# A hybrid SSD and attention block: head products of a group in one cluster, short matmuls first in every other chunk

## The chip, the cores and the metric

The kernel runs on one core of a Trainium2 chip, as one launch. The metric is the device time of that launch in microseconds (us). Weights stay in HBM in float32 and are streamed once.

## The reference

One decoder block over 256 tokens of width 2048, all in float32:

```python
h = rmsnorm(x, norm_w[l])
proj = h @ w_in[l]                       # z | xBC | dt | q k v | g_attn | g_merge
xbc = silu(causal_dwconv(xbc, conv_w[l], conv_b[l]))          # 4 taps
xs, Bm, Cm = jnp.split(xbc, xbc_pts, axis=-1)
dt = softplus(dt_raw + dt_bias[l]); A = -exp(A_log[l])
# ssd_scan, one chunk of 256 tokens, 8 groups of 8 heads of 64 channels:
cum = jnp.cumsum(dt_ * Ah, axis=1)
decay = jnp.exp(jnp.where(causal, cum[l] - cum[s], -jnp.inf))
w = (C @ B.T)[group] * decay * dt        # 256 x 256 for each head
y = w @ x_  +  D_skip * x_
y = group_rmsnorm(y * silu(z), ssm_norm_w[l], 8)
y_ssm = y @ w_ssm_proj[l]
y_attn = (moba_attention(q, k, v) * silu(g_attn)) @ w_attn_proj[l]   # 16 heads, causal softmax
mixed = sigmoid(g_ssm) * y_ssm + sigmoid(g_att) * y_attn
x = rmsnorm(x + mixed @ w_out[l], final_norm_w)
```

## The kernel before

**Weights in chunks.** Every weight matrix is cut into blocks of columns, and each block into chunks of 128 x 1024 numbers (`chunks`, line 103). The main loop (line 903) takes one chunk after another, 480 in all (chunk numbers here count from 0 in the order of the loop). A chunk is loaded on SyncE's queue seven chunks ahead (`load`), and split into two rounded halves for exact enough products: whi on ScalarE four chunks ahead (`split_hi`, line 244), wlo = raw - whi on VectorE, called DVE, three chunks ahead (`split_lo`, line 251). There are five buffers for whi and four for wlo, so DVE's split for chunk n+3 waits until TensorE, called PE, has used the wlo of chunk n-1. The activations (h2 and others) stand in two halves as well.

**Two ways to multiply a chunk.** `by_channel` (line 298) has the weights as stationary operand: eight matmuls of whi against both halves of the activations (128x512, long), and then eight of wlo against the upper half alone (128x256, short). All accumulate in PSUM tiles named acc. It serves z, B and C (bc), x, q, k and the attention gate. `by_token` (line 282) has the activations as stationary operand, 12 long matmuls to a chunk; it serves the gates, v and the three output projections.

**Small work between chunks.** After a chunk's matmuls are issued, `step` advances generators by one yield each: those that empty acc (`evac`), one SSD group (`ssd`, one group at a time) and two attention heads (`attn`). Each engine runs its instructions in the order in which they were issued, so a yield is what sets how many chunks lie between a product and its use. A run of such small matmuls between two chunks is called a cluster here.

**One SSD group** (`ssd_task`, line 541): `xtr(t)` transposes x for one half of the tokens (four matmuls into px); `xmul` scales it by dt on DVE; `decay(p)` takes two heads' differences of cum on DVE and their exp on ScalarE (tile e); `emul(p)` multiplies e by the masked C B (cbm) on DVE; `ymm(p)` multiplies two heads into half a PSUM tile yp with weights of 128x64; `yev(q)` empties one yp on DVE. The four pairs of heads are p = 0 to 3. Later steps multiply by the gate z, take the group's norm with a sum over channels on PE (pn) and write y2, which the SSM projection reads.

Pools that matter: four PSUM tiles for all small products (px, pcb, yp, pn and others) in turn; tag e with three buffers, shared with `rstd_start`; separate tiles for the SSD mask, the attention mask (amask) and rsb (the input norm).

Of the kernel before, what the change touches and what calls it, by code (L numbers as in the profile page):

```python
# [10 lines left out]
F32 = mybir.dt.float32  # L11
F32R = mybir.dt.float32r
AF = mybir.ActivationFunctionType
OP = mybir.AluOpType

P = 128
S = 256
# [3 lines left out]
NG = 8  # L21
# [7 lines left out]
NEG = -1e30  # L29
# [97 lines left out]
def hybrid_block(  # L127
# [12 lines left out]
    nc = tc.nc  # L140
    ctx.enter_context(tc.manual_schedule())

    cpool = ctx.enter_context(tc.tile_pool(name="cpool", bufs=1))
# [3 lines left out]
    pool = ctx.enter_context(tc.tile_pool(name="pool", bufs=1))  # L147
# [48 lines left out]
    for c0 in (0, 256):  # L196
# [1 line left out]
            out=mask[:, c0 : c0 + P], in_=mask[:, c0 : c0 + P], pattern=[[1, P]],  # L198
            compare_op=OP.is_ge, fill=0.0, base=0, channel_multiplier=-1,
        )  # L200

    amask = cpool.tile([P, 384], F32, name="amask")
    nc.gpsimd.memset(amask, 0.0)
    for c0 in (0, 256):
        nc.gpsimd.affine_select(
            out=amask[:, c0 : c0 + P], in_=amask[:, c0 : c0 + P], pattern=[[-1, P]],
            compare_op=OP.is_ge, fill=NEG, base=0, channel_multiplier=1,
        )
    dt_tok = cpool.tile([P, 2, HEADS], F32, name="dt_tok")
    pc_tok = cpool.tile([P, 2, HEADS], F32, name="pc_tok")  # L210
    ssq = cpool.tile([P, 2, 5], F32, name="ssq")
# [67 lines left out]
    def mm(dst, a, bb, start, stop):  # L279
        nc.tensor.matmul(dst, a, bb, start=start, stop=stop, skip_group_check=True)  # L280
# [17 lines left out]
    def by_channel(n, accs):  # L298


        b, k0, per, ncol = cks[n]
        name, _, _, _, row, nrows = blocks[b]
        name = "first" if b < 3 else name
        wh, wl = weights(n, False)
        last_k = nrows // P - 1
        order = [(i, c) for i in range(per) for c in range(ncol // P)]
        passes = [[(part, i, c) for i, c in order] for part in range(2)]
        if len(accs) > 1 and k0 + per > last_k:

            passes = [[x for x in p if x[2] // 2 == a] for a in range(len(accs)) for p in passes]  # L310
        for part, i, c in (x for p in passes for x in p):
            k = k0 + i
            a = operand(name, row // P + k)
            dst = accs[c // 2].rearrange("p (c s) -> p c s", c=2)[:, c % 2]
            cs = slice(c * P, (c + 1) * P)
            if part == 0:
                mm(dst, wh[:, i, cs], a.rearrange("p a s -> p (a s)"), k == 0, False)
            else:
                mm(dst[:, S:], wl[:, i, cs], a[:, 0], False, k == last_k)

# [25 lines left out]
    sq = {}  # L346
# [26 lines left out]

    pss = small("pss")

    rsb = cpool.tile([P, S], F32, name="rsb")

    def init_task():

# [126 lines left out]
    def bc_task(g, acc):  # L506
        bc = pool.tile([P, 2, S], F32, tag="bc", name="bc")
        u = pool.tile([P, 2, S], F32, tag="u", name="u", bufs=2)
        fold(u, acc)
        yield  # L510
        jobs = [(bc[:, i], u[:, i], 32 + 8 * i + g) for i in range(2)]
        for job in jobs:
            tap(*job)
        yield from conv(jobs)
        nc.scalar.activation(bc, bc, AF.Silu)
        yield
        yield
        pcb = small("pcb")
        nc.tensor.matmul(pcb[:, :S], bc[:, 0, :P], bc[:, 1, :], start=True, stop=True)  # L519
        nc.tensor.matmul(pcb[:, S:384], bc[:, 0, P:], bc[:, 1, P:], start=False, stop=True, skip_group_check=True)  # L520
        yield
        cbm = pool.tile([P, 384], F32, tag="s", name="cbm", bufs=2)
        nc.vector.tensor_mul(cbm, pcb[:, :384], mask)
        wk["cbm", g] = cbm

    def x_task(i, acc):
# [14 lines left out]
    def ssd_task(g, xs):  # L541
# [12 lines left out]
        def xtr(t):  # L554
            px[t] = small("px")
            for i in range(4):
                nc.tensor.transpose(px[t][:, i * P : (i + 1) * P], xs[:, i, t * P : (t + 1) * P], ident)  # L557
# [12 lines left out]
        yps = {}  # L570

        def decay(p):
            e = es[p] = pool.tile([P, 2, 384], F32, tag="e", name="e", bufs=3)
            for j in range(2):
                h = 2 * p + j
                hh = g * HPG + h
                cbr = cB[h // 4][:, h % 4]
                for st, sl, dst in ((0, slice(0, S), slice(0, S)), (1, slice(P, S), slice(S, 384))):
                    nc.vector.tensor_scalar(  # L579
                        e[:, j, dst], cbr[:, sl], pc_tok[:, st, hh : hh + 1], 0.0, op0=OP.subtract, op1=OP.max  # L580
                    )
            nc.scalar.activation(e, e, AF.Exp, scale=-1.0)  # L582
# [20 lines left out]
        def yev(q):  # L603
            yp = yps.pop(q)
            for i in (2 * q, 2 * q + 1):
                nc.vector.scalar_tensor_tensor(
                    y[:, i], xs[:, i], dsk[:, 4 * g + i : 4 * g + i + 1], yp[:, (i % 2) * S : (i % 2 + 1) * S],
                    op0=OP.mult, op1=OP.add,
                )

        xtr(0)
        decay(0)
        yield
        xmul(0)
        xtr(1)
        emul(0)
        decay(1)
        yield
# [1 line left out]
        emul(1)  # L620
        decay(2)
        yield
        ymm(0)
        ymm(1)
        emul(2)
        yield
        decay(3)
        yield
        yev(0)
        emul(3)  # L630
        yield
        ymm(2)
        ymm(3)
        yield
        yield
        yev(1)
        yield
# [13 lines left out]
        yield  # L651
        a, r = rstd_start(nc, pool, pn[:, :S], DI // NG, epst)
        yield
        rs = pool.tile([P, S], F32, name="rs")
        rstd_newton(nc, rs, a, r)
        yield
        for i in range(4):
# [8 lines left out]

    SC = 128.0 ** -0.5

    def head_task(u, h, q, k, v, og):
        if h == 1:  # L670
            for _ in range(3):
                yield
        ps = small("ps")
        nc.tensor.matmul(ps[:, :P], q[:, h, :P], k[:, h, :P], start=True, stop=True, skip_group_check=True)  # L674
        nc.tensor.matmul(ps[:, P:384], q[:, h, P:], k[:, h, :], start=False, stop=True, skip_group_check=True)  # L675
        yield
        s = pool.tile([P, 384], F32, tag="s", name="s", bufs=2)
        m = pool.tile([P, 8], F32, name="m", bufs=2)
        nc.vector.tensor_add(s, ps[:, :384], amask)
        nc.vector.reduce_max(m[:, 0:1], s[:, :P], axis=mybir.AxisListType.X)  # L680
        nc.vector.reduce_max(m[:, 1:2], s[:, P:], axis=mybir.AxisListType.X)
        nc.vector.tensor_scalar(m[:, 2:4], m[:, 0:2], -SC, None, op0=OP.mult)
        nc.scalar.activation(s[:, :P], s[:, :P], AF.Exp, bias=m[:, 2:3], scale=SC, accum_out=m[:, 4:5])
        nc.scalar.activation(s[:, P:], s[:, P:], AF.Exp, bias=m[:, 3:4], scale=SC, accum_out=m[:, 5:6])
        yield
        yield
        nc.vector.reciprocal(m[:, 6:8], m[:, 4:6])
        nc.vector.tensor_scalar(s[:, :P], s[:, :P], m[:, 6:7], None, op0=OP.mult)
        nc.vector.tensor_scalar(s[:, P:], s[:, P:], m[:, 7:8], None, op0=OP.mult)
        yield  # L690
        pp = small("pp")
        for i in range(3):
            nc.tensor.transpose(pp[:, i * P : (i + 1) * P], s[:, i * P : (i + 1) * P], ident)  # L693
        yield
        p = pool.tile([P, 384], F32, tag="e", name="p", bufs=3)
        nc.scalar.copy(p, pp[:, :384])
        yield
        po = small("po")
        hs = slice(h * P, (h + 1) * P)

        nc.tensor.matmul(po[:, :S], v[:, 0, hs], p[:, : 2 * P], start=True, stop=False, skip_group_check=True)  # L701
        nc.tensor.matmul(po[:, P:S], v[:, 1, hs], p[:, 2 * P :], start=False, stop=True, skip_group_check=True)  # L702
        yield
        while ("ga", u) not in wk:
            yield
        nc.vector.tensor_mul(og[:, h], po[:, :S], wk["ga", u][:, h])
        if h == 3:
            yield
            both = apool.tile([P, 4, 2, S], F32R, tag="act", name="o2")
            nc.scalar.copy(both[:, :, 0], og)  # L710
            yield
            nc.vector.tensor_sub(both[:, :, 1], og, both.bitcast(F32)[:, :, 0])
            o2[u] = both
# [120 lines left out]
    def residual(acc, j, t, c0, c1, slot):  # L834

        js = slice(j * 512 + c0, j * 512 + c1)
        r = wk["xr"][:, t, js]
        nc.vector.tensor_add(r, acc, r)
        sq = pool.tile([P, 512], F32, tag="e", name="sq", bufs=3)
        nc.scalar.activation(sq[:, : c1 - c0], r, AF.Square, accum_out=ssq[:, t, slot : slot + 1])  # L840
        nc.vector.tensor_mul(r, r, wk["fwt"][:, js])

# [103 lines left out]

def rstd_start(nc, pool, ss, n, epst):

    ar = pool.tile([P, 2, ss.shape[-1]], F32, tag="e", name="ar", bufs=3)
    a, r = ar[:, 0], ar[:, 1]  # L950
    nc.scalar.activation(r, ss, AF.Ln, bias=epst, scale=1.0 / n)
    nc.scalar.activation(r, r, AF.Exp, scale=-0.5)
    nc.vector.tensor_scalar(a, ss, 1.0 / n, EPS, op0=OP.mult, op1=OP.add)
    return a, r
# [45 lines left out]
```

## Time and profile before

| | |
|---|---|
| Time, median of 3 runs | 1433.35 us (1433.32 to 1433.42) |
| Profiled execution, its own time | 1433.54 us |
| Span in the profile | 1431.8 us |
| PE busy | 1414.5 us, 99% |
| DVE busy | 940.1 us, 66% |
| ScalarE (ACT) busy | 768.9 us, 54% |
| DMA, mean rate | 191 GB/s |

Busy times of matmuls overlap, since one starts before the one ahead of it has ended. How fast PE gets on is read from the starts of its rows, not from their durations. The profile shows an engine's wait as idle time before a row, in square brackets with the engine and line that ended it.

### The profile page before, as it was taken

What the parts mean: (1) busy time and instruction counts of PE and PEld (TensorE: products, weight loads), DVE (VectorE), ACT (ScalarE), POOL (GpSimd) and SP (SyncE); (2) the same over time, 40 slices, a digit from 0 to 9 for tenths busy, and PEclk for the clock granted to TensorE, in tenths of its full rate; (3) what the DMA queues carried; (4) which work ended last, traced back from release to release, by engine and by line L of the source; (5) the groups of instructions that cost most, each with busy time, mean ns of one, the idle gap of its engine ahead of it and who ended that gap; (6) DMA issues with size and microseconds to landing.
All of it is one profiled execution on the core that took longest, in us unless ns stands there. A gap on an engine that the chain in (4) does not pass through costs nothing.

```text
span 1431.8 us, 19449 instructions
## 1 busy us (share of the span) xinstructions
PE 1414.5 (99%) x7474; PEld 1204.2 (84%) x7474; DVE 940.1 (66%) x1291; ACT 768.9 (54%) x909; POOL 3.8 (0%) x15
## 2 busy tenths in 40 slices
PE   8999999999999999999999999999999999999997
PEld 7888888888888888888888888888888888888886
DVE  7788788777777777876646555555555555655564
ACT  7556667565756565655444345455454454444352
POOL 0000000000000000000000000000000000000000
PEclk9999999999999999999999999999999999999999
DMA  8455646565656565656665655555655566665762
GB/s 309 146 188 186 212 158 208 164 205 177 216 165 215 168 213 169 200 199 205 206 213 191 188 187 167 186 177 162 192 170 174 186 190 195 203 206 191 262 214 84
DMA packets 77068, 273.66 MB, mean 191 GB/s; under 512 B 8432, under 2 KB 8752, under 8 KB 76592
## 3 DMA queue, kind: packets, MB, share of 16 engines
q1 hardware_dynamic: 76400, 271.68, 58.6%
q8 instruction: 58, 0.95, 0.3%
q10 hardware_dynamic: 576, 0.75, 0.2%
q14 instruction: 34, 0.28, 0.1%
HBM read 270.24 MB, written 2.16 MB: 190 GB/s over the span
## 4 chain that ended last, share of the span: by engine, by line
PE 98%; DVE 1%; DMA 0%; ACT 0%; issue 0%; DVEq 0%; SPq 0%
PE acc L280 92%; PE yp L597 2%; PE half L280 1%; PE px L557 0%; PE po L701 0%; PE ps L675 0%; DMA raw<-wpk 0%; PE pp L693 0%; PE pd L406 0%; PE pcb L519 0%; PE ps L674 0%; PE po L702 0%; PE pm L816 0%; PE pn L650 0%; DVE wlo L251 0%; DVE e L586 0%
## 5 line engine op out<-in xcount | busy, mean ns | idle before, releaser
L251 DVE TENSOR_TENSOR wlo<-raw,whi 128x1024 fp32r<-128x1024 f32 (+1 forms) x477 | 581.4, 1222 | 415.5 <-PE acc L280 315.1
L244 ACT CAST whi<-raw 128x1024 fp32r<-128x1024 f32 (+1 forms) x477 | 496.4, 1046 | 497.2 <-PE acc L280 408.1
L280 PE MATMUL acc<-h,whi 128*128 128x512 f32 x1920 | 489.2, 397 | 0.0
L280 PEld LDWEIGHTS acc<-h,whi 128*128 128x128 f32 x1920 | 346.6, 189 | 65.7 <-issue 2.4
L280 PEld LDWEIGHTS acc<-h,wlo 128*128 128x128 f32 x1920 | 261.8, 190 | 19.2
L280 PE MATMUL acc<-h,wlo 128*128 128x256 f32 x1920 | 267.5, 282 | 0.0
L280 PE MATMUL acc<-whi,h 128*128 128x512 f32 x768 | 241.0, 391 | 0.0
L280 PEld LDWEIGHTS acc<-whi,h 128*128 128x128 f32 x768 | 144.2, 188 | 29.7
L280 PE MATMUL acc<-whi,y 128*128 128x512 f32 x512 | 162.9, 393 | 0.0
L280 PE MATMUL acc<-wlo,h 128*128 128x512 f32 x384 | 149.5, 389 | 0.0
L280 PEld LDWEIGHTS acc<-whi,y 128*128 128x128 f32 x512 | 96.1, 188 | 20.8 <-issue 1.0
L280 PE MATMUL acc<-wlo,y 128*128 128x512 f32 x256 | 99.8, 390 | 0.0
L280 PEld LDWEIGHTS acc<-wlo,h 128*128 128x128 f32 x384 | 72.1, 188 | 14.5
L280 PE MATMUL acc<-whi,o 128*128 128x512 f32 x256 | 79.6, 390 | 0.0
L280 PEld LDWEIGHTS acc<-whi,o 128*128 128x128 f32 x256 | 48.1, 188 | 9.9
L280 PEld LDWEIGHTS acc<-wlo,y 128*128 128x128 f32 x256 | 48.1, 188 | 9.5
L582 ACT ACTIVATE e<-e 128x768 f32<-128x768 f32 x32 | 27.1, 848 | 42.8 <-DVE e L579 42.7
L280 PE MATMUL acc<-wlo,o 128*128 128x512 f32 x128 | 49.8, 389 | 0.0
L499 DVE SCALAR_TENSOR_TENSOR xs<-u,colt,xs 128x255 f32<-128x255 f32 (+2 forms) x96 | 40.7, 478 | 2.1 <-ACT xs L492 2.1
L280 PE MATMUL acc<-wlo,m_hi 128*128 128x512 f32 x104 | 40.6, 390 | 0.0
L280 PE MATMUL acc<-whi,m_hi 128*128 128x512 f32 x104 | 40.5, 390 | 0.0
L280 PE MATMUL acc<-whi,m_lo 128*128 128x512 f32 x104 | 40.5, 389 | 0.0
(192 smaller groups left out, 1044.6 us busy)
## 6 DMA issues: line engine op xcount, KB each, us to landing
raw<-wpk SPq DMA_DIRECT2D x479, 512.0 KB, 3.6
cumb<-scratch SPq DMA_DIRECT2D x16, 512.0 KB, 6.1
sig<-gbias SPq DMA_DIRECT2D x8, 512.0 KB, 6.8
xt<-xT SPq DMA_DIRECT2D x8, 256.0 KB, 6.9
xr<-x SPq DMA_DIRECT2D x1, 2048.0 KB, 11.3
out<-xr SPq DMA_DIRECT2D x6, 256.0 KB, 3.6
fwt<-fw SPq DMA_DIRECT2D x1, 1024.0 KB, 12.4
raw<-wpk SPq DMA_DIRECT2D x2, 256.0 KB, 6.3
```

The source lines that it names most:

```text
L244: nc.scalar.copy(his[n][:, h], raws[n][:, h])
L251: nc.vector.tensor_sub(los[n][:, h], r[:, h], his[n].bitcast(F32)[:, h])
L280: nc.tensor.matmul(dst, a, bb, start=start, stop=stop, skip_group_check=True)
L499: nc.vector.scalar_tensor_tensor(dst[:, d:], u[:, : S - d], cw[:, ct, 3 - d : 4 - d], dst[:, d:], op0=OP.mult, op1=OP.add)
L582: nc.scalar.activation(e, e, AF.Exp, scale=-1.0)
L597: nc.tensor.matmul(yp[r, st * P :], xd[:, st, h * 64 : (h + 1) * 64], e[:, j, :S] if st == 0 else e[:, j, S:384], start=(st == 0 and p % 2 ...
```

## The change

1. Both x transposes of a group stand in one cluster, and all four `ymm` as well: four pairs of heads, behind one more yield. The tag e gets a fourth buffer.
2. In `by_channel` every chunk with an odd place in its block does its short matmuls (wlo) first and its long ones after.
3. To make room, the attention mask is written over the SSD mask when the last group has used it (`attn_mask`), and rsb and each group's rs share one buffer.

```diff
@@ by_channel
+        turn = (0, 1) if k0 // per % 2 == 0 else (1, 0)
-        passes = [[(part, i, c) for i, c in order] for part in range(2)]
+        passes = [[(part, i, c) for i, c in order] for part in turn]
...
-                mm(dst, wh[:, i, cs], a.rearrange("p a s -> p (a s)"), k == 0, False)
+                mm(dst, wh[:, i, cs], a.rearrange("p a s -> p (a s)"), k == 0, k == last_k)
@@ init and ssd_task
-    rsb = cpool.tile([P, S], F32, name="rsb")
+    rsb = pool.tile([P, S], F32, tag="rs", name="rsb", bufs=1)
...
-            e = es[p] = pool.tile([P, 2, 384], F32, tag="e", name="e", bufs=3)
+            e = es[p] = pool.tile([P, 2, 384], F32, tag="e", name="e", bufs=4)
...
         xtr(0)
+        xtr(1)
         decay(0)
         yield
         xmul(0)
-        xtr(1)
         emul(0)
         decay(1)
         yield
...
         emul(1)
         decay(2)
         yield
-        ymm(0)
-        ymm(1)
         emul(2)
-        yield
         decay(3)
         yield
+        emul(3)
+        yield
+        yield
+
+        for p in range(4):
+            ymm(p)
+        yield
+        yield
         yev(0)
-        emul(3)
-        yield
-        ymm(2)
-        ymm(3)
-        yield
         yield
         yev(1)
...
-        rs = pool.tile([P, S], F32, name="rs")
+        rs = pool.tile([P, S], F32, tag="rs", name="rs", bufs=1)
@@ masks
+        if g == NG - 1:
+            attn_mask()
...
+    def attn_mask():
+
+        nc.gpsimd.memset(mask, 0.0)
+        for c0 in (0, 256):
+            nc.gpsimd.affine_select(
+                out=mask[:, c0 : c0 + P], in_=mask[:, c0 : c0 + P], pattern=[[-1, P]],
+                compare_op=OP.is_ge, fill=NEG, base=0, channel_multiplier=1,
+            )
...
-        nc.vector.tensor_add(s, ps[:, :384], amask)
+        nc.vector.tensor_add(s, ps[:, :384], mask)
```

On PE, in SSD group 0, from the product pcb of the next group's B and C to the head products yp, before (two of the four pairs stand here, the other two stood three chunks earlier, ahead of pcb):

```order
L519 MATMUL pcb<-bc 128x256
L520 MATMUL pcb<-bc 128x128
L280 MATMUL acc<-h_123,whi 128x512 x8
L280 MATMUL acc<-h_123,wlo 128x256 x8
L280 MATMUL acc<-h_123,whi 128x512 x8
L280 MATMUL acc<-h_123,wlo 128x256 x8
L280 MATMUL acc<-h_123,whi 128x512 x8
L280 MATMUL acc<-h_123,wlo 128x256 x8
L597 MATMUL yp<-e,xd 64x256 x2
L597 MATMUL yp<-e,xd 64x128 x2
L597 MATMUL yp<-e,xd 64x256 x2
L597 MATMUL yp<-e,xd 64x128 x2
```

The same stretch of PE in the changed kernel:

```order
L513 MATMUL pcb<-bc 128x256
L514 MATMUL pcb<-bc 128x128
L272 MATMUL acc<-h_115,wlo 128x256 x8
L272 MATMUL acc<-h_115,whi 128x512 x16
L272 MATMUL acc<-h_115,wlo 128x256 x16
L272 MATMUL acc<-h_115,whi 128x512 x8
L593 MATMUL yp<-e,xd 64x256 x2
L593 MATMUL yp<-e,xd 64x128 x2
L593 MATMUL yp<-e,xd 64x256 x2
L593 MATMUL yp<-e,xd 64x128 x2
L593 MATMUL yp<-e,xd 64x256 x2
L593 MATMUL yp<-e,xd 64x128 x2
```

Two more pairs (four more rows of the same two kinds) follow there; all four pairs now stand where the last two stood, and runs of long and of short matmuls join across chunks.

On DVE, group 0, from the fourth `decay` to its `emul` (the product e<-e,cbm), before:

```order
L579 TENSOR_SCALAR e<-cumb,pc_tok 128x256
L579 TENSOR_SCALAR e<-cumb,pc_tok 128x128
L579 TENSOR_SCALAR e<-cumb,pc_tok 128x256
L579 TENSOR_SCALAR e<-cumb,pc_tok 128x128
L251 TENSOR_TENSOR wlo<-raw,whi 128x1024
L523 TENSOR_TENSOR cbm<-pcb,mask 128x384
L499 SCALAR_TENSOR_TENSOR xs<-u,colt,xs 128x254
L499 SCALAR_TENSOR_TENSOR xs<-u,colt,xs 128x253 x2
L606 SCALAR_TENSOR_TENSOR y<-xs,colt,yp 128x256 x2
L586 TENSOR_TENSOR e<-e,cbm 128x768
```

And now:

```order
L575 TENSOR_SCALAR e<-cumb,pc_tok 128x256
L575 TENSOR_SCALAR e<-cumb,pc_tok 128x128
L575 TENSOR_SCALAR e<-cumb,pc_tok 128x256
L575 TENSOR_SCALAR e<-cumb,pc_tok 128x128
L243 TENSOR_TENSOR wlo<-raw,whi 128x1024
L493 SCALAR_TENSOR_TENSOR xs<-u,colt,xs 128x255 x2
L493 SCALAR_TENSOR_TENSOR xs<-u,colt,xs 128x254
L582 TENSOR_TENSOR e<-e,cbm 128x768
L243 TENSOR_TENSOR wlo<-raw,whi 128x1024
L517 TENSOR_TENSOR cbm<-pcb,mask 128x384
L493 SCALAR_TENSOR_TENSOR xs<-u,colt,xs 128x254
L493 SCALAR_TENSOR_TENSOR xs<-u,colt,xs 128x253 x2
```

The fourth `emul` moved up past the second split, cbm and three taps; y<-xs,colt,yp (`yev`) moved behind them.

On PE at the start of the program, chunks 0 to 2, before:

```order
L280 MATMUL acc<-hp,whi 128x512 x8
L280 MATMUL acc<-hp,wlo 128x256 x8
L280 MATMUL acc<-hp,whi 128x512 x8
L280 MATMUL acc<-hp,wlo 128x256 x8
L280 MATMUL acc<-hp,whi 128x512 x8
L280 MATMUL acc<-hp,wlo 128x256 x8
```

And chunks 0 to 4 now, with the first half of chunk 5:

```order
L272 MATMUL acc<-hp,whi 128x512 x8
L272 MATMUL acc<-hp,wlo 128x256 x16
L272 MATMUL acc<-hp,whi 128x512 x16
L272 MATMUL acc<-hp,wlo 128x256 x16
L272 MATMUL acc<-hp,whi 128x512 x16
L272 MATMUL acc<-hp,wlo 128x256 x16
```

Chunk 1 now begins with its wlo.

## Rows read from the trace of the kernel before

**Rows 1.** The page: the span, and PE's busy time.

```profile
span 1431.8 us, 19449 instructions
PE 1414.5 (99%) x7474; PEld 1204.2 (84%) x7474; DVE 940.1 (66%) x1291; ACT 768.9 (54%) x909; POOL 3.8 (0%) x15
```

**Rows 2.** PE's waits: who for whom, us in total, times, longest.

```profile
PE yp L597 <- DVE e L586: 3.5, 3, 1.2
```

**Rows 3.** PE's timeline, plain chunks: start us, us, instruction.

```profile
13.02 1.12 PE L280 MATMUL acc<-hp,wlo 128*128 128x256 f32 x8
...
24.20 1.12 PE L280 MATMUL acc<-hp,wlo 128*128 128x256 f32 x8
```

**Rows 4.** PE's timeline, long matmuls alone, then short ones alone.

```profile
1384.66 0.39 PE L280 MATMUL acc<-whi,m_hi 128*128 128x512 f32 x1
...
1397.35 0.39 PE L280 MATMUL acc<-whi,m_lo 128*128 128x512 f32 x1
...
1411.35 0.40 PE L280 MATMUL half<-last,m_hi 128*128 128x256 f32 x2
...
1417.11 0.40 PE L280 MATMUL half<-last,m_hi 128*128 128x256 f32 x2
```

**Rows 5.** PE's timeline, x transposes of group 0, then of group 3.

```profile
114.97 1.12 PE L280 MATMUL acc<-h,wlo 128*128 128x256 f32 x8
115.93 0.60 PE L557 MATMUL px<-ident,xs 128*128 128x128 f32 x4
116.29 2.10 PE L280 MATMUL acc<-h,whi 128*128 128x512 f32 x8
118.22 1.11 PE L280 MATMUL acc<-h,wlo 128*128 128x256 f32 x8
...
302.21 0.62 PE L280 MATMUL acc<-whi,y 128*128 128x512 f32 x2
...
306.11 0.39 PE L280 MATMUL acc<-whi,y 128*128 128x512 f32 x1
```

**Rows 6.** PE's timeline, head products of group 0 and, below, group 4.

```profile
134.94 1.11 PE L280 MATMUL acc<-h,wlo 128*128 128x256 f32 x8
...
138.01 0.87 PE L597 MATMUL yp<-e,xd 128*64 128x256 f32 x8 [1.16 <-DVE e L586]
...
140.75 1.12 PE L280 MATMUL acc<-h,wlo 128*128 128x256 f32 x8
...
398.85 1.11 PE L280 MATMUL acc<-h,wlo 128*128 128x256 f32 x8
399.89 1.52 PE L597 MATMUL yp<-e,xd 128*64 128x256 f32 x16
...
403.32 1.10 PE L280 MATMUL acc<-h,wlo 128*128 128x256 f32 x8
```

**Rows 7.** DVE's timeline in group 0.

```profile
133.44 1.22 DVE L251 TENSOR_TENSOR wlo<-raw,whi 128x1024 fp32r<-128x1024 f32 x1
...
137.00 0.95 DVE L586 TENSOR_TENSOR e<-e,cbm 128x768 f32<-128x768 f32 x1
```

**Rows 8.** Timeline of the start, DVE and PE.

```profile
11.07 1.23 DVE L251 TENSOR_TENSOR wlo<-raw,whi 128x1024 fp32r<-128x1024 f32 x1 [0.52 <-ACT whi L244]
11.09 2.10 PE L280 MATMUL acc<-hp,whi 128*128 128x512 f32 x8
...
33.73 3.06 PE L280 MATMUL acc<-hp,whi 128*128 128x512 f32 x8 [2.39 <-DVE z L329]
...
38.15 1.99 PE L280 MATMUL acc<-hp,whi 128*128 128x512 f32 x8
```

**Rows 9.** Windows: stretch, its us, PE busy, granted clock, DMA share, GB/s.

```profile
34.60:37.90 3.30, 3.30 (x13) 0.50 0.84 335
```

**Rows 10.** PE's timeline, the first two pd clusters.

```profile
46.60 1.68 PE L406 MATMUL pd<-xt,wd 128*64 128x256 f32 x8
...
54.00 1.08 PE L406 MATMUL pd<-xt,wd 128*64 128x256 f32 x8
```

More of the change, by code (lines that the diff above doesn't have):

```diff
@@ L200, in hybrid_block @@
         )
[L202 to L208, printed above, removed]
     dt_tok = cpool.tile([P, 2, HEADS], F32, name="dt_tok")
@@ L622, in ssd_task @@
         yield
-        ymm(0)
-        ymm(1)
         emul(2)
-        yield
         decay(3)
         yield
-        yev(0)
         emul(3)
         yield
-        ymm(2)
-        ymm(3)
         yield
+        for p in range(4):
+            ymm(p)
+        yield
+        yield
+        yev(0)
         yield
@@ L694, in head_task @@
         yield
-        p = pool.tile([P, 384], F32, tag="e", name="p", bufs=3)
+        p = pool.tile([P, 384], F32, tag="e", name="p", bufs=4)
         nc.scalar.copy(p, pp[:, :384])
@@ L838, in residual @@
         nc.vector.tensor_add(r, acc, r)
-        sq = pool.tile([P, 512], F32, tag="e", name="sq", bufs=3)
+        sq = pool.tile([P, 512], F32, tag="e", name="sq", bufs=4)
         nc.scalar.activation(sq[:, : c1 - c0], r, AF.Square, accum_out=ssq[:, t, slot : slot + 1])
@@ L947, in rstd_start @@
 def rstd_start(nc, pool, ss, n, epst):
-    ar = pool.tile([P, 2, ss.shape[-1]], F32, tag="e", name="ar", bufs=3)
+    ar = pool.tile([P, 2, ss.shape[-1]], F32, tag="e", name="ar", bufs=4)
     a, r = ar[:, 0], ar[:, 1]
```

## The prediction

> **What bounds the kernel now.** I read the page first. TensorE (PE) is busy 99% of the span, 1414.5 of 1431.8 us [rows 1]; the others have far more room and PE hardly waits. So the time is the sum of the spacings between PE's matmuls, and only what changes that sum can move it. The view of waits names what PE waits for; the one row that the change touches is the wait of the head products (yp, line 597) for DVE's e, three times [rows 2]. Everything else is spacing, read from the starts in PE's timeline, because the busy times of pipelined matmuls overlap.
>
> **Four spacings.** (1) A plain chunk of by_channel (8 long matmuls on whi, 8 short on wlo): 13.02 to 24.20 is four chunks, 2.795 us each [rows 3]. (2) In a stretch of long ones alone, 1384.66 to 1397.35, 56 steps of one matmul each take 12.69 us, 0.2266 us a step; in 48 short ones alone, 1411.35 to 1417.11, a step is 0.120 us [rows 4]. Eight of each would be 2.773 us, so a plain chunk pays 0.02 us for its two changes of length. (3) A cluster of four x transposes between short and long matmuls: 114.97 to 118.22 is 3.25 us where a plain chunk takes 2.79, so it costs 0.46 us. Between long ones it is dearer: 302.21 to 306.11 holds 15 long matmuls (3.40 us), so the cluster costs 0.50 us [rows 5]. (4) A cluster of head products of two pairs (two passes each, 16 rows): 398.85 to 403.32 is 4.47 us, a cost of 1.68; the one that waits, 134.94 to 140.75, is 5.81 us, a cost of 3.02 [rows 6].
>
> **The change, part by part.**
>
> *All four pairs in one cluster.* Sixteen matmul rows last 1.52 us and eight last 0.87 [rows 6], so eight more cost 0.65 and a cluster of 32 costs 1.68 + 1.30 = 2.98 us in place of 2 x 1.68 = 3.36. That is 0.38 us for each of 8 groups: **3.0 us**. What goes is one entry and one exit. The bounds are 0 (ends cost nothing) and 8 x 0.5 = 4. The three pcb clusters that followed yp without a break now stand alone or elsewhere; I take nothing for that, and at worst one more entry and exit each, 3 x 0.38 = 1.1. The Trainium skill, "TensorEngine Tiling (Array Packing)", section Key Properties, says that a change of tiling mode, unlike a change of tile, drains TensorE. yp loads weights of 128x64 where its neighbours load 128x128. By that rule alone the yp merge pays and the merge of the x transposes, which are 128x128 like their neighbours, is worth nothing: the sum below would be 10.4 us. The rows agree on yp and put a little on the transposes as well (next but one part).
>
> *The wait for e.* In groups 0 to 2 the second pair of pairs waited for the last product with the mask: 3.02 - 1.68 = 1.34 us each, **4.0 us** together. In the new order that product stands on DVE ahead of a weight split, cbm, three convolution taps and yev, which in the old trace fill 133.44 to 137.00 [rows 7], and PE comes to it two chunks later instead of one. For group 0 I follow it by hand: without those 3.56 us it would end near 134.4, plus up to 1.7 us because ScalarE must now do the fourth exp before the taps: 136.1. PE reaches the new cluster near 134.2 (135.98 less the cluster of 1.68 us that no longer stands ahead of it and some 0.1) and its last pair 3 x 0.65 us later, 136.1. So group 0 just about fits, groups 1 and 2 have a further chunk. Bounds: all 4.0 gone, or 1.34 kept.
>
> *x transposes together.* Two clusters cost 0.92 us; four more transposes cost at least 0.36, the distance from the first one to the next long matmul (115.93 to 116.29), and at most the whole 0.46 [rows 5]: eight cost 0.82 to 0.92. I take 0.88, nearer to the upper end as the last transpose of a cluster overlaps what follows: 0.04 saved, 8 times, **0.3 us**.
>
> *Short matmuls first in every other chunk.* There are 256 such chunks, so 128 pairs of length changes go: 128 x 0.02 = 2.6 us. Against it, clusters that used to stand between short and long now stand half between long and long, which costs 0.50 rather than 0.46 for px; by the order there are about 34 such places: 34 x 0.04 = 1.3 us back. The other half stand between short and short, which the trace doesn't show: nothing, as a short step is 0.120 us in any run [rows 3, 4], to 37 x 0.04 = 1.5 us. I take nothing there: **1.3 us**, between -0.2 and 2.6.
>
> *The start.* Chunk 1 now begins with wlo, which DVE writes from 11.07 to 12.30, while PE began that chunk at 11.09 [rows 8]: a new wait of 1.2 us. It is paid out of a wait that is there already: PE stands 2.39 us before 33.73 until the first z is folded, and in the order of issue that fold comes behind splits of later chunks on ScalarE and DVE, so I take it that PE being 1.2 us later doesn't hold it up. So the end of the start doesn't move (cost 0; 1.2 if that cover were gone), and the idle stretch shrinks to about 1.2 us. After the 2.39 us the clock was granted at 0.50 (1.2 GHz) in 34.6 to 37.9 [rows 9], and that chunk lasted 33.73 to 38.15, 4.42 us, against 2.79 and some 0.1 for the cold entry: 1.5 us. The idle 1.16 us before 138.01 had no such sequel: that cluster's whole excess of 1.34 us lies before 140.75, in the gap itself [rows 6]. With two gaps of 1.2 instead of one of 2.39 I expect full clock: **1.5 us**; bounds 1.5 gained or, if the new gap at 11 to 12.3 brings a slow stretch of its own that the shorter gap hides in part, 0.4 lost.
>
> *Decay sums pd.* The first pd cluster lasts 1.68 us, the next 1.08 [rows 10]; it is strung out because xt comes one by one from DVE, whose splits wait for PE to free wlo. Chunk 9 now frees wlo first, so DVE is about 1 us earlier: **0.6 us**, bounds 0 and 0.6.
>
> *No cost taken:* the fourth e buffer, rsb and rs in one place (rsb's readers end before group 0's rs), and the attention mask written over the SSD mask (idle POOL, after the last cbm near chunk 189, read from chunk 281 on). If a reader were late, one wait of some us.
>
> **Sum.** 3.0 + 4.0 + 0.3 + 1.3 + 1.5 + 0.6 = 10.7 us. The profiled execution took 1433.54 us (span 1431.8), 0.19 above the median of the runs, 1433.35. So 1433.35 - 10.7 = 1422.7 us.
>
> **Rivals.**
> - *The clock falls all the same* (one of the two gaps suffices): the sum without 1.5 us, 1424.2. For it: the row of 0.50 follows a gap only twice as long. Chance 0.27.
> - *A wait takes the old one's place*: the last pair waits for e in groups 0 to 2 after all, or a small PSUM tile isn't free because both yp now hold two of four buffers until yev. At the full old price, 4.0 us: 1426.7; with the clock fallen too, 1428.2. Against it: the hand count above fits, and yp's second buffer was px's, read six steps earlier. Chance 0.12. The Trainium skill, "TensorEngine Tiling (Array Packing)", section PSUM Bottleneck, names such a danger: where TensorE gets faster, emptying PSUM can become the limit. No row here shows PE waiting for yp to be emptied.
> - *The order of passes gives nothing or costs*: short-short clusters at their upper bound and the pairs' gain spent, 1.5 less: 1424.2 to 1425.7. Chance 0.06.
> - *Slower than before*: every short-first chunk needs its wlo 1.8 us earlier than now. If DVE's splits came too late throughout, each of the 128 would wait; from 10.7 / 128 = 0.084 us each the gain is gone, and at 0.11 us it is 1436.7, slower by over 0.2%. For it: it does happen at chunk 1. Against it: the split at 133.44 is, by the order, for chunk 41, whose first matmul comes after 140.75 [rows 6, 7], over 6 us later. Chance 0.04.
> - *Nothing measurable*: the gains on paper are absorbed by something that I have not seen, within 2.9 us of 1433.35. Chance 0.08.
>
> **Numbers.** The forecast, all terms with the clock held, has 0.43: 1422.7, its own range 1421 to 1424. The range of all cases that leaves out no more than 2 in 10 reaches from 1420.8 (short-long changes worth the full 2.6, entry and exit 0.5) to 1427.2, most of the case with waits kept. A change of 0.2%, 2.9 us, is about what a measurement of this kernel can tell from none. Faster by more: 0.43 + 0.27 + 0.12 + 0.06 = 0.88, as even 1428.2 is 5 us below. Within: 0.08. Slower: 0.04.
>
> **What the new profile would show.** PE's timeline: yp clusters of 32 matmul rows without an idle bracket, and two neighbouring chunks with 16 short and 16 long rows in about 5.57 us. The waits: no yp row; one for wlo near 11. The windows near 34 to 38 with clock 1.00. First pd cluster near 1.08 us. The prediction is wrong if yp rows show idle time before them, if 16 short matmuls run slower than 0.120 us each, or if DVE's splits appear among PE's waits beyond chunk 1.

## The result and the profile after

The changed kernel takes 1424.21 us (median of 5, 1422.72 to 1424.23) where the one before takes 1433.35 beside it (5 runs): 0.9937 of it, with an interval of 0.9925 to 0.9948, or 9.1 us less. The profiled execution was the quickest of the five, 1422.72 us. To read the numbers below one needs to know that the times of both kernels fall in groups about 1.5 us apart, without and with a stretch of half clock near 34 us (a few of the kernel before lie another 1.5 to 2 us higher), so where terms of a microsecond are compared, I name the group: "full clock" or "with the stretch".

The page, against [rows 1]: the span is 10.8 us shorter, PE is still busy 99% of it, and the count of matmuls is the same.

```profile
span 1421.0 us, 19512 instructions
PE 1406.2 (99%) x7474; PEld 1201.9 (85%) x7474; DVE 938.3 (66%) x1291; ACT 768.0 (54%) x908; POOL 4.1 (0%) x15
```

PE's waits (us in total, times, longest), against [rows 2]: the wait of yp for e is gone. The new wait for wlo is there, and the one for the first z is 2.0 us.

```profile
PE acc L272 <- DVE z L323: 2.0, 1, 2.0
...
PE acc L272 <- DVE wlo L243: 1.4, 1, 1.4
```

PE's timeline (start us, us, instruction, idle time before it and what ended it): the start, then group 0's head products, and the rows on either side of those of another group.

```profile
12.14 1.22 PE L272 MATMUL acc<-hp,wlo 128*128 128x256 f32 x8 [1.42 <-DVE wlo L243]
...
18.76 3.82 PE L272 MATMUL acc<-hp,whi 128*128 128x512 f32 x16
...
24.33 3.82 PE L272 MATMUL acc<-hp,whi 128*128 128x512 f32 x16
...
31.75 0.59 PE L380 MATMUL pss<-total,ones 128*128 128x256 f32 x2
34.34 2.09 PE L272 MATMUL acc<-hp,whi 128*128 128x512 f32 x8 [2.00 <-DVE z L323]
...
41.83 2.08 PE L272 MATMUL acc<-hp,wlo 128*128 128x256 f32 x16
...
45.67 1.08 PE L400 MATMUL pd<-xt,wd 128*64 128x256 f32 x8
...
130.90 2.00 PE L272 MATMUL acc<-h,whi 128*128 128x512 f32 x8
132.84 2.82 PE L593 MATMUL yp<-e,xd 128*64 128x256 f32 x32
...
137.53 2.08 PE L272 MATMUL acc<-h,wlo 128*128 128x256 f32 x16
...
195.19 1.11 PE L272 MATMUL acc<-h,wlo 128*128 128x256 f32 x8
...
200.04 3.82 PE L272 MATMUL acc<-h,whi 128*128 128x512 f32 x16
```

Read the starts. Two plain chunks, 18.76 to 24.33, take 5.57 us, as forecast, against 2 x 2.795 [rows 3]. The yp cluster has no idle bracket: 130.90 to 137.53 less 16 long steps of 0.2266 us leaves 3.00 us for it between long matmuls, and 195.19 to 200.04 less 16 short steps of 0.120 us leaves 2.93 between short ones; 2.98 was forecast. (From 195.19 to 200.04 stand 8 short ones, the cluster and 8 short ones.) The first pd cluster lasts 1.08 us, not 1.68 [rows 10]. Chunk 8, though, which began at 33.73 in [rows 8], now begins at 34.34: the gap ahead of it has shrunk by 0.39 us only, and the fold ends later.

The last product with the mask of group 0 ends on DVE at 134.27, and the last pair of the cluster begins at about 134.7. So it fits by some 0.4 us, where the prediction's count by hand had both at 136.1.

```profile
133.32 0.95 DVE L582 TENSOR_TENSOR e<-e,cbm 128x768 f32<-128x768 f32 x1
```

The window of [rows 9] in this execution (stretch, its us, PE busy, granted clock, DMA share, GB/s) was at full clock:

```profile
34.60:37.90 3.30, 3.30 (x22) 1.00 0.73 290
```

Why the fold is late shows on ScalarE and DVE. First the kernel before, then the changed one:

```profile
30.75 0.59 PE L386 MATMUL pss<-total,ones 128*128 128x256 f32 x2
31.32 1.04 ACT L244 CAST whi<-raw 128x1024 fp32r<-128x1024 f32 x1 [1.28 <-DMA raw<-wpk]
32.89 1.29 DVE L329 TENSOR_TENSOR z<-acc,z 128x512 f32<-128x512 f32 x2
```

```profile
31.94 1.04 ACT L236 CAST whi<-raw 128x1024 fp32r<-128x1024 f32 x1 [2.05 <-PE acc L272]
32.90 1.07 ACT L322 COPY z<-acc 128x512 f32<-128x512 f32 x2
33.51 1.29 DVE L323 TENSOR_TENSOR z<-acc,z 128x512 f32<-128x512 f32 x2 [0.69 <-ACT z L322]
```

ScalarE copies z for the fold only behind the split for chunk 12. That split waited for its DMA before; now it waits for PE. By the code it needs the whi buffer of chunk 7 (five buffers), and chunk 7 now uses its whi last, so the buffer comes free only when the chunk ends, near 31.75.

### The profile page after: what moved, and what is told of

It reads as the page before. It is cut to its first block, busy times and chain, and to the rows that moved or that the text cites. A ratio compares the mean times of both kernels' runs of the same rounds, so it can differ in the third digit from the quotient of the medians.

```text
span 1421.0 us, 19512 instructions
## 1 busy us (share of the span) xinstructions
PE 1406.2 (99%) x7474; PEld 1201.9 (85%) x7474; DVE 938.3 (66%) x1291; ACT 768.0 (54%) x908; POOL 4.1 (0%) x15
## 4 chain that ended last, share of the span: by engine, by line
PE 98%; DMA 0%; ACT 0%; DVE 0%; SPq 0%; issue 0%; DVEq 0%
PE acc L272 92%; PE yp L593 2%; PE half L272 1%; PE px L553 0%; PE ps L680 0%; PE po L706 0%; DMA raw<-wpk 0%; PE pp L698 0%; PE pd L400 0%; PE pcb L513 0%; PE ps L679 0%; PE po L707 0%; PE pm L821 0%; PE pn L646 0%; ACT whi L236 0%; PE pcb L514 0%
## 5 line engine op out<-in xcount | busy, mean ns | idle before, releaser
L272 PE MATMUL acc<-h,whi 128*128 128x512 f32 x1920 | 468.6, 393 | 0.0
L272 PEld LDWEIGHTS acc<-h,whi 128*128 128x128 f32 x1920 | 351.2, 188 | 68.6 <-issue 1.5
L272 PE MATMUL acc<-h,wlo 128*128 128x256 f32 x1920 | 258.8, 285 | 0.0
L272 PEld LDWEIGHTS acc<-h,wlo 128*128 128x128 f32 x1920 | 248.9, 191 | 10.7 <-issue 0.7
```

## The experiments

**Theory:** at equal clock the terms are those of the forecast and add up; the start took 0.6 us back, because the fold does depend on PE, and the clock falls or holds by chance after a gap of 2 us. **Rivals:** the wait for e alone made the gain, and merging clusters and joining runs gave nothing; or the late fold is DVE's or the DMA's, not PE's; or the two groups of times have nothing to do with the gap.

### The order of passes alone

The kernel before, with short matmuls first in odd chunks from the fourth block on:

```diff
-        passes = [[(part, i, c) for i, c in order] for part in range(2)]
+        turn = (1, 0) if b > 2 and k0 // per % 2 else (0, 1)
+        passes = [[(part, i, c) for i, c in order] for part in turn]
...
-                mm(dst, wh[:, i, cs], a.rearrange("p a s -> p (a s)"), k == 0, False)
+                mm(dst, wh[:, i, cs], a.rearrange("p a s -> p (a s)"), k == 0, k == last_k)
```

> The kernel before with one edit: every other chunk does its short matmuls first, but only from the fourth block of columns on (240 of the 256 chunks), so that the start of the program stays as it was. The waits for e and the clusters stay too. By the prediction's sum the order of passes is worth 240 / 256 of 1.3 us net of the clusters that come to stand between long matmuls, so 1.2 us (bounds -0.2 and 2.4): 1432.1 us. Rival: the order is worth nothing, 1433.35 us; a second rival, that clusters between short runs are cheaper too, would bring it to the upper bound, 1431 us.

Measured: 1431.58 us against 1433.49, ratio 0.9987 (0.9979 to 0.9996), so 1.9 us. The wait for e stays, as PE's waits show:

```profile
PE yp L598 <- DVE e L587: 3.6, 3, 1.2
PE acc L280 <- DVE z L330: 2.6, 1, 2.6
```

The order of passes is worth something by itself. The interval, 0.6 to 3.0 us, leaves out zero but does not tell 1.3 from 1.9 or 2.6. The traces do (behind the last experiment): 1.8 us.

### The clusters alone

The changed kernel with every chunk long first:

```diff
-        turn = (0, 1) if k0 // per % 2 == 0 else (1, 0)
+        turn = (0, 1)
```

> The changed kernel with long matmuls first in every chunk, as before. What is left is the merge of the clusters, the moved product and the shared buffers. By the prediction's sum: 3.0 for one cluster of four pairs, 4.0 for the waits, 0.3 for the x transposes, so 7.3 us less than before: 1426.0 us, with the slow clock near 34 us and the long first pd cluster of before. Rival: the merge of clusters is worth nothing and only the waits went: 1429.3 us.

Measured: 1425.96 us, ratio 0.9949 (0.9937 to 0.9962). That the median meets the 1426.0 is luck, for of the five times this one alone stands in that group: two are at full clock, and two (1427.54 and 1427.60) some 1.6 us above it. At full clock it is 1424.46 and 1424.70 against 1431.88 and 1432.09 of before in the same series: 7.4 us. With the 1.9 of the order alone that is 9.3, and the changed kernel at full clock is 9.3 below (below, last experiment): the parts add up. The profiled execution of this kernel (1427.60) shows the gap, and half clock from 33.09, still inside the gap, to 39.91, longer than in [rows 9]:

```profile
33.82 3.75 PE L272 MATMUL acc<-hp,whi 128*128 128x512 f32 x8 [2.74 <-DVE z L323]
```

```profile
33.09:39.91 6.82, 6.09 (x18) 0.50 0.56 216
```

### Two clusters of head products, neither of them waiting

```diff
+        ymm(0)
+        ymm(1)
         yield
-
-        for p in range(4):
-            ymm(p)
+        ymm(2)
+        ymm(3)
```

> The changed kernel with the head products in two clusters of two pairs again, one chunk apart, the second where the merged one stands; the product with the mask stays early, so that e should be there. It tells the wait from the merge. If a merged cluster saves an entry and an exit of 0.38 us for each of 8 groups, this is 3.0 us slower than the changed kernel. Rival: the ends of a cluster cost nothing and all of the gain on yp was the wait: no difference.

Measured: 1426.97 us, ratio 0.9954 (0.994 to 0.9968), 2.8 above the changed kernel; at full clock 1425.40 and 1425.52 against 1422.72, 2.7 above (2.9 by the traces, behind the last experiment). PE's timeline in group 0:

```profile
128.78 1.11 PE L272 MATMUL acc<-h,wlo 128*128 128x256 f32 x8
129.83 1.52 PE L593 MATMUL yp<-e,xd 128*64 128x256 f32 x16
...
132.34 2.00 PE L272 MATMUL acc<-h,whi 128*128 128x512 f32 x8
134.27 1.52 PE L593 MATMUL yp<-e,xd 128*64 128x256 f32 x16
...
137.66 2.08 PE L272 MATMUL acc<-h,wlo 128*128 128x256 f32 x16
```

No wait stands here, and the two clusters cost 3.56 - 1.92 = 1.64 and 5.32 - 3.63 = 1.69 us, 3.33 together, against 3.00 for the one: 0.33 us in this group, and 2.9 / 8 = 0.36 over all. So the merge pays apart from the wait.

### Long and short matmuls one by one

The changed kernel, with the two passes interleaved in each chunk of the later blocks:

```diff
+        if b > 2:
+            passes = [[(part, i, c) for i, c in order for part in turn]]
```

> The changed kernel, but from the fourth block on each chunk takes long and short matmuls in turn, one by one: 16 changes of length in a chunk in place of one. If a change of length costs 0.01 us each (0.02 for the two of a plain chunk), this is 240 x 15 x 0.01 = 36 us slower. Rival: the loss sits in the first long matmuls after a run of short ones, which has used up what was loaded ahead; a single short one among long ones then costs no more than its own 0.114 us and the long one 0.227 to 0.233 us, which makes the chunk 2.73 to 2.77 us and the kernel up to 5 us faster than the changed one, or about equal.

Measured: 1427.57 us, ratio 0.9958 (0.9945 to 0.997); 1426.05 at full clock, 3.3 above the changed kernel. Both expectations were wrong. PE's timeline:

```profile
112.03 0.40 PE L272 MATMUL acc<-h,whi 128*128 128x512 f32 x1
112.27 0.28 PE L272 MATMUL acc<-h,wlo 128*128 128x256 f32 x1
112.38 0.40 PE L272 MATMUL acc<-h,whi 128*128 128x512 f32 x1
...
114.14 0.40 PE L272 MATMUL acc<-h,whi 128*128 128x512 f32 x1
```

Six pairs take 2.11 us from 112.03 to 114.14, 0.352 a pair; eight would be 2.81 where a plain chunk in two passes takes 2.795. Against the 2.773 of eight and eight without a change, sixteen changes of length cost 0.04 us and two cost 0.02. So a change has no fixed price: a long matmul behind a short one takes 0.24 us here instead of 0.2266 (112.03 to 112.27), the short one behind it 0.11 instead of 0.120 (112.27 to 112.38), and so most of the loss comes back at once. The rival had the loss in the right place, but not its size.

### Chunk 1 long first

The start undone, the rest kept:

```diff
-        turn = (0, 1) if k0 // per % 2 == 0 else (1, 0)
+        turn = (0, 1) if n == 1 or k0 // per % 2 == 0 else (1, 0)
```

> The changed kernel with one chunk turned back: chunk 1 does its long matmuls first, so that nothing waits for its wlo. In the changed kernel's profile that wait is 1.42 us, and the fold of the first z comes 0.6 us later than before, because ScalarE's split for chunk 12 needs the whi buffer of chunk 7, which short-first order gives back only at the chunk's end. If that is the chain, chunk 7 ends 1.2 us earlier here, the split waits for its weights again and the fold comes some 0.6 us earlier: 1423.6 us. Rival: the fold doesn't depend on PE at all, as the prediction had it: no difference, 1424.2 us.

Measured: 1422.20 us, ratio 0.9927 (0.9915 to 0.994). Timeline:

```profile
31.12 0.59 PE L380 MATMUL pss<-total,ones 128*128 128x256 f32 x2
31.32 1.04 ACT L236 CAST whi<-raw 128x1024 fp32r<-128x1024 f32 x1 [1.57 <-PE acc L272]
33.72 2.09 PE L272 MATMUL acc<-hp,whi 128*128 128x512 f32 x8 [2.00 <-DVE z L323]
```

PE reaches pss 0.63 us earlier than in the changed kernel, the split follows 0.62 earlier, chunk 8 0.62 earlier, and the gap is 2.00 us as in the changed kernel: between these two the fold moves one for one with PE. Three of the five times, 1421.99 to 1422.20, are 0.6 below the changed kernel's full-clock ones. The expected 1423.6 was for the group with the stretch; the two times there, 1423.88 and 1423.94, are only 0.3 below the changed kernel's, so it is the trace, and not the median, that decides between the chain and its rival.

### The fold ahead of the splits

`evac` steps once before the splits are issued at chunk 8, in the changed kernel; then the same with chunk 1 long first; then the same in the kernel before:

```diff
         load(n + PF)
+        if n == 8:
+            step(evac)
...
-        step(evac)
+        if n != 8:
+            step(evac)
```

> The changed kernel, but at chunk 8 the first z is folded before ScalarE and DVE take up the splits for later chunks. PE stands 2.00 us there in the changed kernel. If the wait is one of order on ScalarE and DVE, it shrinks to 0.3 us or less, and if the slow clock near 34 us, which most executions have, comes of that gap, it is gone too: 1424.2 - 1.7 - 1.5 = 1421.0 us in nearly all executions. Rival: the slow clock comes of something else (the wait at chunk 1, say) and stays: 1422.5 us in most executions.

> Both edits: z folded first at chunk 8, and long matmuls first in chunk 1. With the later gap closed, the wait at chunk 1 is no longer covered, so taking it away is now worth its own 1.2 us: 1419.8 us. Rival: weights arrive no faster than that and PE waits elsewhere in the first 30 us: the same as with the fold alone, 1421.0 us.

> The kernel before with the fold of the first z taken first at chunk 8, and nothing else. PE stands 2.39 us there before. If that gap is what brings the slow clock near 34 us, both go here too: 1433.4 - 2.2 - 1.5 = 1429.7 us in all executions. Rival: the slow clock in the kernel before has another cause, and only the gap goes: 1431.2 us in most executions.

Measured for the first: 1420.61 us (1420.56 to 1420.79), ratio 0.9912 (0.9898 to 0.9926), quicker than both kernels and 0.4 below what was expected. PE's timeline has no gap left:

```profile
31.68 0.59 PE L380 MATMUL pss<-total,ones 128*128 128x256 f32 x2
32.27 2.11 PE L272 MATMUL acc<-hp,whi 128*128 128x512 f32 x8
```

With chunk 1 long first as well: 1420.61 again, ratio 0.9912 (0.9898 to 0.9925). The expected 1419.8 was wrong. The time is the rival's, that of the fold alone, but the gain is lost later than in the rival's first 30 us: PE is 0.6 us earlier at pss there and then waits for the fold, which stands behind DVE's earlier splits (two of them, 29.16 to 31.51):

```profile
29.16 2.35 DVE L243 TENSOR_TENSOR wlo<-raw,whi 128x1024 fp32r<-128x1024 f32 x2
...
31.09 0.59 PE L380 MATMUL pss<-total,ones 128*128 128x256 f32 x2
31.43 1.27 DVE L323 TENSOR_TENSOR z<-acc,z 128x512 f32<-128x512 f32 x2
32.17 2.11 PE L272 MATMUL acc<-hp,whi 128*128 128x512 f32 x8 [0.49 <-DVE z L323]
```

In the kernel before: 1430.70 us (1430.52 to 1430.87, 11 runs), ratio 0.9986 (0.9977 to 0.9995). Chunk 8 begins at 32.40 instead of 33.73, 1.33 us earlier, and that is the gain against the full-clock times of before beside it (1431.75 to 1432.15, 7 of 15). Its expectation counted on the whole gap and was 1 us too low; the rival's 1431.2 was nearer. Two things stand against the whole gap here. DVE's earlier splits hold the fold up, as in the kernel just shown, where chunk 8 begins no earlier than 32.17. And the first chunk of this execution ran at half clock, so that PE came to pss 1.0 us later than in the kernel before (31.73 against 30.75):

```profile
7.62:11.03 3.41, 3.24 (x8) 0.50 1.03 416
```

Which of the two set the 1.33 isn't shown.

The other thing that these three show: all their 19 times lie in one group, within 0.4 us for each kernel, and none of the three profiled executions has half clock near 34 us. Without the gap that stretch, and its 1.5 us, did not come.

### The x transposes apart

```diff
         xtr(0)
-        xtr(1)
         decay(0)
         yield
         xmul(0)
+        xtr(1)
```

> The changed kernel with the two x transposes of a group in clusters of their own again, one chunk apart. The spacing of rows before and after (0.44 to 0.50 us for four, 0.87 to 0.90 for eight) gives 0.4 us more in all: 1424.6 us. Rival, by the rule that only a change of tiling mode costs something: no difference.

Measured: 1424.43 us, ratio 0.9934 (0.9921 to 0.9948): 0.2 above the changed kernel, 0.3 at full clock (1422.97 and 1423.03 against 1422.72). That leans to the forecast, but as a time it is about the limit of what can be told; the traces say 0.4 (behind the last experiment). This kernel's profiled execution is of use for the clock too, for it has the changed kernel's gap to the hundredth:

```profile
34.21 2.52 PE L272 MATMUL acc<-hp,whi 128*128 128x512 f32 x8 [2.00 <-DVE z L323]
...
43.20 2.08 PE L272 MATMUL acc<-hp,wlo 128*128 128x256 f32 x16
```

```profile
35.00:38.00 3.00, 3.00 (x13) 0.61 0.69 274
```

From chunk 8 to the same row of short matmuls it takes 34.21 to 43.20, 8.99 us, where the changed kernel takes 34.34 to 41.83, 7.49. The stretch costs 1.50 us, and after the same 2.00 us of idle time it came here and did not come there.

### The changed kernel again

No edit; five more runs, beside before with the fold first.

> The changed kernel once more, unedited, beside the kernel before on the same chip, to count in how many executions the slow clock near 34 us appears. If it falls by chance after the gap of 2.0 us, its times stand in two groups again, near 1422.7 and 1424.2 us; if the first count of four in five was peculiar to one chip, nearly all times are near 1422.7 us.

Measured: 1424.10 us, ratio 0.9937 (0.9924 to 0.9949), with 1422.53 and 1422.87 as the quick ones. With the first series, 3 of 10 executions kept the clock, judged by their times (the two that were profiled both kept it). At full clock it is 9.3 below before (means of 1422.70 and of 1431.98, the 7 times from 1431.75 to 1432.15), with the stretch 9.2.

Times can't part terms of some tenths, but the traces can. From the first pd cluster to the last pm cluster (transposes of the mixed result, near the end) the start and the stretch near 34 us play no part, and executions whose code differs only at the start agree there to 0.02 us (the kernel before with and without the fold first; the changed kernel twice, and its three variants of the start). PE's rows: pm in the kernel before (pd at 46.60 in [rows 10]), then pd and pm in the order alone and in the clusters alone, pm in the changed kernel (pd at 45.67, above), then pd and pm in the two clusters and in the transposes apart:

```profile
1339.56 1.03 PE L816 MATMUL pm<-ident,mix 128*128 128x128 f32 x8
...
44.94 1.68 PE L407 MATMUL pd<-xt,wd 128*64 128x256 f32 x8
1336.06 1.03 PE L817 MATMUL pm<-ident,mix 128*128 128x128 f32 x8
...
47.92 1.69 PE L400 MATMUL pd<-xt,wd 128*64 128x256 f32 x8
1333.64 1.03 PE L821 MATMUL pm<-ident,mix 128*128 128x128 f32 x8
...
1328.77 1.03 PE L821 MATMUL pm<-ident,mix 128*128 128x128 f32 x8
...
45.47 1.08 PE L400 MATMUL pd<-xt,wd 128*64 128x256 f32 x8
1331.48 1.03 PE L822 MATMUL pm<-ident,mix 128*128 128x128 f32 x8
...
47.05 1.08 PE L400 MATMUL pd<-xt,wd 128*64 128x256 f32 x8
1330.53 1.03 PE L821 MATMUL pm<-ident,mix 128*128 128x128 f32 x8
```

| Kernel | pd to pm, us | Difference |
|---|---|---|
| before | 1292.96 | |
| order alone | 1291.12 | 1.84 less than before |
| clusters alone | 1285.72 | 7.24 less than before |
| changed | 1283.10 | 9.86 less than before |
| two clusters | 1286.01 | 2.91 more than changed |
| transposes apart | 1283.48 | 0.38 more than changed |

So the order of passes is worth 1.8 us, the merge of the head products 2.9 and that of the transposes 0.4.

## Why the prediction was right, and which step failed

The direction and the size are right: the median, 1424.21, lies in the range of all cases, 1.5 us above the forecast and just outside the forecast's own 1421 to 1424. It stands where the rival "the clock falls all the same" put it, with a chance of 0.27 against 0.43. In full-clock executions the forecast's 1422.7 is met (1422.53 to 1422.87). That it is met to the tenth is luck: the order of passes gave some 0.6 us more than forecast, and the start took 0.6 that the forecast had at nothing.

- **All pairs in one cluster, 3.0:** right, 2.9 measured with the wait taken away from both sides. The single cluster costs what was forecast (2.93 to 3.00 against 2.98). The two that it replaces are a little cheaper where one of them stands between short matmuls, 1.64 rather than 1.68. The Trainium skill, "TensorEngine Tiling (Array Packing)", section Key Properties, says that a change of tiling mode drains TensorE. A merge that leaves the number of matmuls as it was and still saves 0.36 us agrees with that, and so does the little (0.05 us) that a merge of the transposes saves, which are 128x128 like their neighbours; that a drain is the cause isn't shown.
- **The wait for e, 4.0:** right. The row is gone from the waits. Of the 7.24 us of the clusters alone, less 2.91 for the merge and 0.38 for the transposes, 3.9 are left for it. No run takes away the wait and nothing else, so this is a difference, and the two terms taken off were measured in the other order of passes.
- **x transposes, 0.3:** right, 0.4 by the traces.
- **Order of passes, 1.3:** mis-sized. For the 240 chunks that the order alone turns, 1.2 was forecast and 1.8 measured, inside the bounds. The term at fault is probably the one that I took at nothing, the clusters between short matmuls. The same cluster of two pairs costs 1.64 us between short ones, 1.68 between short and long [rows 6] and 1.69 between long ones. So what clusters lose in one place they regain in another. That this is the 0.6 us is argued. The picture behind the term, a price for each change of length, was wrong (interleaving).
- **pd, 0.6:** right, 1.68 became 1.08; it stayed 1.68 and 1.69 in the order alone and in the clusters alone, where the early chunks are long first.
- **The start, cost 0:** wrong. The step that failed is "I take it that PE being 1.2 us later doesn't hold it up". The wait for wlo is there, 1.4 us, and PE reaches pss 1.0 us later than before (31.75 against 30.75). The fold stands behind a split that waits for a buffer which a short-first chunk frees later, and comes 0.6 us later. I looked at which instructions stand ahead of the fold, but not at what each of them waits for. The cost, 0.6 us, cancels the gain at pd.
- **The clock near 34 us, 1.5:** the price was right (1.50) and the step failed with the one above. I expected the gap to shrink from 2.39 to about 1.2; it shrank to 2.00, and in 7 of 10 executions, judged by their times, the half clock still followed. With the gap gone it did in none of 19, judged the same way.
- **The other rivals** did not come about: no wait in the old one's place, no splits among PE's waits beyond chunk 1 in the changed kernel.

At full clock the terms as measured are 2.9 + 3.9 + 0.4 + 1.8 + 0.6 - 0.6 = 9.0 us, against 9.3 by the times; for the 0.3 left over no run accounts. The 3.9 is what was left of the clusters' 7.24, so this sum tests only that the clusters, the order and the start add up.

## What to carry to other kernels

When an engine that is busy 99% of its span is to do the same work, count spacings: the ends of clusters (0.36 us for each pair of clusters of head products merged here), waits, and the order in which work of different shape stands. Before calling a delay hidden by a wait that is there already, follow what ends that wait back through its queue, and ask of each instruction ahead of it what buffer it needs and whose progress frees it. An idle stretch of the engine that sets the time costs its own length and may cost the clock behind it, so removing it can be worth more than the stretch (2.1 us of gap and 1.5 of clock here, by one reordering of issue).

## What the runs showed of the hardware that was not expected

- Changing between 512 and 256 columns with every matmul, 16 times a chunk, costs hardly more than changing twice: 2.81 against 2.795 us. The loss sits in the long ones behind short ones, 0.24 us against 0.2266 in a stretch of long ones alone [rows 4], and the short ones give most of it back, 0.11 against 0.120.
- The same cluster takes less between short matmuls than between long ones: 2.93 against 3.00 us for all four pairs, 1.64 against 1.69 for two. Of the 0.07 some part is the change from short to long, which falls into the second stretch alone.
- The clock after an idle stretch is not decided by that stretch alone: after the same 2.00 us it was granted at 1.00 in one execution and fell to half in another, and in the order alone, after 2.6 us, it was granted at 1.00 from 33.5 to 40. Half clock came elsewhere too: from 7.62 to 11.03 in the kernel before with the fold first, after 2.28 us of idle time ahead of chunk 0, where the kernel before kept full clock after 1.49 us. What else decides it stays open.
